# Dealing TensorE's score matmuls out in a fixed order around the gate matmuls

## The chip, the core and the metric

The kernel runs on one core of a Trainium2 chip. The metric is the device time of one execution in microseconds; lower is better. The engines are TensorE (PE in the profile; PEld is its weight load), VectorE (DVE), ScalarE (ACT), GpSimd (POOL), and SyncE (SP), which only issues transfers here. An engine takes its own instructions in the order in which they stand in its queue; what can be reordered is done when the program is built.

## The reference

One decoder layer for 512 tokens of width 1024. The part that matters is the expert mixer at its end (`xb` is the normed input, `T` tokens, 8 heads, 128x128 single-neuron experts, top 16 of them per head):

```python
q = (xb @ w_query).reshape(t, 8, 2, 128)
scores = jnp.einsum("thpc,hpkc->thpk", q, sk)
s1, i1 = lax.top_k(scores[:, :, 0], 16)
s2, i2 = lax.top_k(scores[:, :, 1], 16)
cand = s1[..., :, None] + s2[..., None, :]         # 256 pairs; idx = i1 * 128 + i2
top_s, top_pos = lax.top_k(cand, 16)
gate = jax.nn.softmax(top_s, axis=-1)
act = gelu(einsum("td,thkd->thk", xb, expert_down[idx]))
out = einsum("thk,thkd->td", gate * act, expert_up[idx])
```

## The kernel before

Of the four blocks of 128 tokens, one gathers its experts' rows. The other three (384 tokens, `TD`) are computed densely, and the change touches them alone. For a row `i` of 128 experts the dense way needs three things: the scores `h = gelu(down_i @ xn)` for 128 experts x 384 tokens, the gates `g` (the softmaxed gate of a token where it chose the expert, else zero), and `acc += (h * g).T @ up_i`. There are 128 such rows.

**Score tiles** (`s_tile`, L623). SyncE loads 512 KB of the down table into `w_raw`; ScalarE rounds it to `w_hi` (L615); GpSimd computes the rest `w_lo = w_raw - w_hi` (L616, `load_pair`); TensorE runs 24 matmuls into `s_ps`, eight steps of three (L125 to L127 through `mm3`); ScalarE applies the gelu into `h_act` or `h_far` (L633, L630). `w_raw`, `w_hi`, `w_lo` and `s_ps` have two buffers each. 46 score tiles are made ahead of the accumulation (`make_ahead`, L639): seven between the query heads (L756), nine more after the last head (L757), thirty during the gates (L806). The other 82 are made during the accumulation.

**Selection.** VectorE finds the top 16 of each head (`topk`), then the softmax runs over VectorE and ScalarE (`softmax`, L705: subtract, `Exp` on ScalarE at L708, sum, reciprocal, multiply into `ex`). Nine transposes on TensorE (L763), three each of `i1a`, `i2a` and `ex`, turn the indices and gates so that a token is a column.

**Gates** (L776 to L806). The 384 tokens are taken four at a time, a quad: 96 quads in twelve groups of eight. For a quad, one-hot matrices `oa` and `ob` are built (128x128 per token, four buffers each): on VectorE (L794, L796), or, for two quads of ten, `oa` on ScalarE (L789, L790, an `Abs` and a `Relu` per token) and `ob` on VectorE (L785). TensorE multiplies them into `g_ps` (L800, four fp32 matmuls, which the profile counts as eight passes; six buffers), and ScalarE copies the result into the staging tile `stg` (L801). `stg` has one buffer and holds a group: after its eighth copy GpSimd copies a small part to `gsb0` (L804), SyncE writes the rest to `gmat` in DRAM (L805, 1984 KB), and only then may the next group's first copy write `stg`.

**Accumulation** (L890 on). For each row `i`, VectorE multiplies `h` by the gates into `w` (L902), `w` is split into `whi` and `wlo`, and TensorE runs 18 matmuls into `acc` (L885). The gates of the first four rows come from `gsb0`, later ones are read back from `gmat`.

**What sets the order.** Nothing in this kernel writes out the order between score matmuls and gate matmuls: a scheduler merges the streams engine by engine with estimates of its own, and the pools decide how far it may run ahead. `tc.issue_after(ins)` puts the instructions traced under it behind `ins` in the queue of `ins`'s engine; it is an order in the queue, not a semaphore wait.

Of the kernel before, what the change touches and what calls it, by code (L numbers as in the profile page):

```python
# [12 lines left out]
AF = mybir.ActivationFunctionType  # L13
# [5 lines left out]
P = 128  # L19
T = 512  # L20
D = 1024
DC = D // P
# [9 lines left out]
NG = 1  # L32
NDT = NTB - NG
TD = NDT * P
TG = 32
NTG = TD // TG
# [4 lines left out]
FAR = 20  # L41
S_QUERY = 7
S_WAIT = 9
AHEAD = RUN + FAR
LEAD = 4
FAR_TILES = [RUN + ((2 * k + 1) * (NK - RUN)) // (2 * FAR) for k in range(FAR)]
# [25 lines left out]
def hymba_peer_block(ctx, tc, consts, x, nmix, w_in, w_ba, conv_w, a_log, dt_bias, dn_w, w_pool, pool_scale,  # L72
                     w_out, nffn, w_q, sub_k, downT, down, up, nfin, out):
    nc = tc.nc
# [5 lines left out]
    ident = cst[:, C_ID:C_ID + P]  # L80
# [41 lines left out]
    def mm3(ps, a, b, first, last):  # L122
        ahi, alo = a
        bhi, blo = b
        nc.tensor.matmul(ps, ahi, bhi, start=first, stop=False)  # L125
        nc.tensor.matmul(ps, ahi, blo, start=False, stop=False)  # L126
        nc.tensor.matmul(ps, alo, bhi, start=False, stop=last)  # L127

    def transpose_split(h, tb, hi, lo, psp):
        for q in range(2):  # L130
# [17 lines left out]
    with ExitStack() as fx:  # L148
# [82 lines left out]
        with tc.tile_pool(name="prep", bufs=1) as pr:  # L231
# [58 lines left out]
            for h in range(DNH):  # L290
                for qk, dst in ((0, qT), (1, kT)):
# [84 lines left out]
        with ExitStack() as f2:  # L376
# [110 lines left out]
            for tb in range(NTB):  # L487
# [32 lines left out]
                for h in range(DNH):  # L520
                    nc.tensor.matmul(ops[:, tsl(h)], d["aq"][:, h], vn[:, h], start=(tb == 0 and h == 0),
                                     stop=(h == 3))
# [96 lines left out]
    def h_slot(i):  # L619
        h_tiles[i] = hp[i % (RUN + 1) >= RA].tile([P, TD], F32, name="h_act")  # L620
        return h_tiles[i]

    def s_tile(i, eng):  # L623
        hi, lo = load_pair(downT[i], eng)
        ps = ps_s.tile([P, 512], F32, name="s_ps")[:, :TD]
        for c in range(DC):
            mm3(ps, (hi[:, c, :], lo[:, c, :]), (xn_hi[:, c, NG * P:], xn_lo[:, c, NG * P:]), c == 0, c == DC - 1)
        if i in FAR_TILES:
            ht = hq.tile([P, TD], F32, name="h_far")
            nc.scalar.activation(ht, ps, AF.Gelu)  # L630
            nc.sync.dma_start(out=hfar[FAR_TILES.index(i)], in_=ht)
        else:
            nc.scalar.activation(h_slot(i), ps, AF.Gelu)  # L633


    ahead = list(range(RUN)) + FAR_TILES
# [2 lines left out]
    def make_ahead(goal):  # L639
        while made[0] < min(goal, AHEAD):  # L640
            s_tile(ahead[made[0]], nc.gpsimd)
            made[0] += 1


    def refill(i):
# [56 lines left out]
            nc.vector.tensor_reduce(dst, oh[:, p], axis=AX.X, op=ALU.add)  # L702
        yield

    def softmax(pool, dst, sc):  # L705
        n = sc.shape[1]
        nc.vector.tensor_sub(dst, sc, sc[:, :, 0:1].broadcast_to([P, n, K]))
        nc.scalar.activation(dst, dst, AF.Exp)  # L708
        sm = pool.tile([P, n], F32, name="sm", bufs=1)
        nc.vector.tensor_reduce(sm, dst, axis=AX.X, op=ALU.add)  # L710
        nc.vector.reciprocal(sm, sm)
        nc.vector.tensor_tensor(dst, dst, sm[:, :, None].broadcast_to([P, n, K]), op=ALU.mult)

    with ExitStack() as fy:
        tk = fy.enter_context(tc.tile_pool(name="tk", bufs=2))
        p_pj = fy.enter_context(tc.tile_pool(name="p_pj2", bufs=2, space=PSUM))
        p_sc = fy.enter_context(tc.tile_pool(name="p_sc", bufs=4, space=PSUM))
        skt = tk.tile([P, 16, NK], F32, name="skt", bufs=1)
        nc.scalar.dma_start(out=skt, in_=sub_k)
        SA = [P, NDT, PH, K]  # L720
        i1a = tk.tile(SA, F32, name="i1a", bufs=1)
        i2a = tk.tile(SA, F32, name="i2a", bufs=1)
        tsa = tk.tile(SA, F32, name="tsa", bufs=1)

        def query(h, eng):
            qh = tk.tile([P, 2, T], F32, name="qh")
            w = [load_pair(w_q[2 * h + p], eng) for p in range(2)]
            ps = [p_pj.tile([P, 512], F32, name="q_ps") for p in range(2)]
            parts = [slice(0, T)] if h else [slice(0, T // 2), slice(T // 2, T)]
            for ts in parts:  # L730
                for p in range(2):
                    for c in range(DC):
                        mm3(ps[p][:, ts], (w[p][0][:, c, :], w[p][1][:, c, :]), (xn_hi[:, c, ts], xn_lo[:, c, ts]),
                            c == 0, c == DC - 1)
            for p in range(2):
                cp = nc.scalar.copy(qh[:, p], ps[p])
            behind[:] = [None, cp.ins]
            sc = tk.tile([P, NDT, 2, NK], F32, name="sc")
            ps = [p_sc.tile([P, 512], F32, name="sc_ps") for _ in range(NTB)]
            for p in range(2):  # L740
                for tb in range(NTB):
                    nc.tensor.matmul(ps[tb][:, p * NK:(p + 1) * NK], qh[:, p, tb * P:(tb + 1) * P],
                                     skt[:, 2 * h + p, :], start=(p == 0), stop=(p == 1))
            for tb in range(NTB):
                nc.scalar.copy(sc0[:, tb, h] if tb < NG else sc[:, tb - NG],
                               ps[tb][:, :2 * NK].rearrange("p (a k) -> p a k", a=2))
            return sc

        sc = query(0, nc.vector)
        for h in range(PH):  # L750
            sc_next = query(h + 1, nc.gpsimd) if h + 1 < PH else None
            for _ in topk(tk, sc, NDT, tsa[:, :, h, :], i1a[:, :, h, :], i2a[:, :, h, :]):
                pass
            sc = sc_next
            if sc is not None:
                make_ahead(h + 1)  # L756
        make_ahead(S_QUERY + S_WAIT)  # L757
        ex = tk.tile(SA, F32, name="ex", bufs=1)
        softmax(tk, ex.rearrange("p b h k -> p (b h) k"), tsa.rearrange("p b h k -> p (b h) k"))
        for src, dst in ((i1a, i1t), (i2a, i2t), (ex, gtt)):  # L760
            ps = p_pj.tile([P, 512], F32, name="q_ps")
            for b in range(NDT):
                nc.tensor.transpose(ps[:, b * P:(b + 1) * P], src[:, b].rearrange("p h k -> p (h k)"), ident)  # L763
            nc.vector.tensor_copy(dst, ps[:, :TD])
            if dst is not i2t:
                nc.scalar.activation(n1t if dst is i1t else ngt, ps[:, :TD], AF.Copy, scale=-1.0)
# [3 lines left out]
    with ExitStack() as fy:  # L770
        hq = fy.enter_context(tc.tile_pool(name="hq", bufs=2))
        gs = fy.enter_context(tc.tile_pool(name="gs", bufs=3))
        p_g = fy.enter_context(tc.tile_pool(name="p_g", bufs=6, space=PSUM))
        gsb0 = gp.tile([P, NTG, GN * TG], F32, name="gsb")
        ng = 0
        for tg in range(NTG):  # L776
            stg = gs.tile([P, NK, TG], F32, name="stg", bufs=1)
            for q in range(TG // 4):
                oa = gs.tile([P, 4, P], F32, name="oa", bufs=4)
                ob = gs.tile([P, 4, P], F32, name="ob", bufs=4)  # L780
                ps = p_g.tile([P, 512], F32, name="g_ps")
                t0 = tg * TG + q * 4
                q4 = [P, 4, P]
                if ng % 10 in A_ACT:
                    nc.vector.tensor_tensor(ob, iota[:, None, :].broadcast_to(q4),  # L785
                                            i2t[:, t0:t0 + 4, None].broadcast_to(q4), op=ALU.is_equal)
                    for u in range(4):
                        t = t0 + u
                        nc.scalar.activation(oa[:, u], iota, AF.Abs, bias=n1t[:, t:t + 1])  # L789
                        nc.scalar.activation(oa[:, u], oa[:, u], AF.Relu, scale=ngt[:, t:t + 1], bias=gtt[:, t:t + 1])  # L790
                else:
                    for u in range(4):
                        t = t0 + u
                        nc.vector.tensor_scalar(ob[:, u], iota, i2t[:, t:t + 1], gtt[:, t:t + 1], op0=ALU.is_equal,  # L794
                                                op1=ALU.mult)
                    nc.vector.tensor_tensor(oa, iota[:, None, :].broadcast_to(q4),  # L796
                                            i1t[:, t0:t0 + 4, None].broadcast_to(q4), op=ALU.is_equal)
                ng += 1
                for u in range(4):
                    nc.tensor.matmul(ps[:, u * P:(u + 1) * P], ob[:, u], oa[:, u], start=(u == 0), stop=(u == 3))  # L800
                nc.scalar.copy(stg[:, :, q * 4:q * 4 + 4].rearrange("p i t -> p t i"),  # L801
                               ps.rearrange("p (t i) -> p t i", i=NK))
            sv = stg.rearrange("p i t -> p (i t)")
            nc.gpsimd.tensor_copy(gsb0[:, tg, :], sv[:, :GN * TG])  # L804
            nc.sync.dma_start(out=gmat[tg, :, GN * TG:], in_=sv[:, GN * TG:])  # L805
            make_ahead(S_QUERY + S_WAIT + (tg + 1) * (AHEAD - S_QUERY - S_WAIT) // NTG)  # L806

    with ExitStack() as fz:
        fin = fz.enter_context(tc.tile_pool(name="fin", bufs=1))
# [182 lines left out]
```

## Time and profile before

| | us |
|---|---|
| median of three runs | 1635.62 (1633.59 to 1635.65) |
| the profiled execution | 1633.33, of which the span of the trace is 1631.6 |
| TensorE busy | 1550.3 (95%) |
| VectorE, ScalarE, GpSimd busy | 1258.6, 706.1, 573.1 |
| from the last query to the first `acc` matmul | about 431.5 to 746.5 on the span |

The span starts with the first instruction of the trace; all times in the text are counted from there. "Busy" adds up instruction times, so an engine can be busy and slow (TensorE at a lower clock), or idle for a short stretch that a share of the whole span hides. For that the profile is read by stage: how long TensorE stood in a stretch, and which engine's event ended the wait.

### The profile page before, as it was taken

How to read it: one execution, taken by the hardware profiler on the slowest of the kernel's cores; microseconds unless marked ns; L12 is line 12 of the kernel's file. 1: busy time of each engine (PE TensorE's matmuls, PEld its weight loads, DVE VectorE, ACT ScalarE, POOL GpSimd, SP SyncE). 2: the span in 40 equal slices, each digit the busy share in tenths (PEclk: the TensorE clock that was granted, in tenths of full speed). 3: DMA queues.
4: the chain of work that ended last, by engine and by line, in shares of the span. 5: the costliest groups of instructions: out<-in, count | busy, mean ns of one | idle time of the engine just before them, and what ended most of it. 6: DMA issues, size and time to landing. Idle time of an engine off the chain costs nothing.

```text
span 1631.6 us, 23412 instructions
## 1 busy us (share of the span) xinstructions
PE 1550.3 (95%) x8417; PEld 1393.4 (85%) x8417; DVE 1258.6 (77%) x2666; ACT 706.1 (43%) x1097; POOL 573.1 (35%) x389
## 2 busy tenths in 40 slices
PE   6999999999949899999999999999999999999996
PEld 5888898888948888889888898888888888888885
DVE  5576646799967666668989888788888888888985
ACT  5545344333326877773333333333333333333333
POOL 2003230144433333330045444455444444444431
PEclk9999999999979999999999999999999999999998
DMA  6221221423313445557589989999999999999982
GB/s 205 78 65 54 66 79 40 161 90 98 92 52 128 165 174 189 189 189 240 171 309 344 388 309 344 349 333 328 336 344 340 323 338 333 337 322 347 335 274 88
DMA packets 140661, 364.97 MB, mean 224 GB/s; under 512 B 11040, under 2 KB 63792, under 8 KB 138880
## 3 DMA queue, kind: packets, MB, share of 16 engines
q1 hardware_dynamic: 102544, 224.98, 39.8%
q0 software_dynamic: 37856, 137.44, 23.2%
q8 instruction: 66, 1.08, 0.3%
q10 hardware_dynamic: 144, 1.05, 0.2%
q14 instruction: 51, 0.42, 0.1%
HBM read 330.40 MB, written 33.03 MB: 223 GB/s over the span
## 4 chain that ended last, share of the span: by engine, by line
PE 84%; DVE 6%; issue 4%; DMA 3%; ACT 2%; POOL 1%; SPq 0%; ACTq 0%; DVEq 0%; POOLq 0%
PE acc L885 30%; PE s_ps L127 10%; PE s_ps L125 10%; PE s_ps L126 10%; PE pj L125 3%; PE pj L126 3%; PE pj L127 3%; PE g_ps L800 2%; PE q_ps L126 2%; PE q_ps L127 2%; PE q_ps L125 2%; DVE ob L794 1%; ACT stg L801 1%; PE ups L435 1%; PE p L444 1%
## 5 line engine op out<-in xcount | busy, mean ns | idle before, releaser
L125 PE MATMUL s_ps<-xn_hi,w_hi 128*128 128x384 f32 x1024 | 351.7, 343 | 20.4 <-ACT h_act L633 20.1
L127 PE MATMUL s_ps<-xn_hi,w_lo 128*128 128x384 f32 x1024 | 348.1, 340 | 2.9 <-POOL w_lo L616 2.9
L126 PE MATMUL s_ps<-xn_lo,w_hi 128*128 128x384 f32 x1024 | 347.9, 340 | 0.0
L615 ACT ACTIVATE w_hi<-w_raw 128x1024 fp32r<-128x1024 f32 x144 | 152.6, 1060 | 322.4 <-PE s_ps L126 234.6
L860 POOL DMA_INDIRECT row<-in_down_dram,eidx x128 | 180.8, 1413 | 263.3 <-DVE row L862 160.2
L869 POOL DMA_INDIRECT row<-in_up_dram,eidx x128 | 177.1, 1383 | 211.6 <-DVE xr L871 183.9
L885 PE MATMUL acc<-u_lo,whi 128*128 128x512 f32 x768 | 237.7, 389 | 2.1 <-DVE u_lo L120 2.1
L885 PE MATMUL acc<-u_hi,whi 128*128 128x512 f32 x768 | 238.4, 391 | 0.0
L885 PE MATMUL acc<-u_hi,wlo 128*128 128x512 f32 x768 | 237.4, 389 | 0.0
L616 POOL TENSOR_TENSOR w_lo<-w_raw,w_hi 128x1024 fp32r<-128x1024 f32 x60 | 149.1, 2486 | 244.2 <-ACT w_hi L615 216.8
L125 PEld LDWEIGHTS s_ps<-xn_hi,w_hi 128*128 128x128 f32 x1024 | 193.7, 189 | 24.3 <-ACT h_act L633 20.4
L127 PEld LDWEIGHTS s_ps<-xn_hi,w_lo 128*128 128x128 f32 x1024 | 193.7, 189 | 3.8 <-POOL w_lo L616 3.8
L119 ACT ACTIVATE whi<-w 128x384 fp32r<-128x384 f32 x128 | 67.1, 525 | 298.5 <-issue 250.3
L126 PEld LDWEIGHTS s_ps<-xn_lo,w_hi 128*128 128x128 f32 x1024 | 193.6, 189 | 3.2
L862 DVE SCALAR_TENSOR_TENSOR row<-row,xg 128x1024 f32<-128x1024 f32 x128 | 153.2, 1221 | 26.8 <-DMA row<-in_down_dram,eidx 26.5
L885 PEld LDWEIGHTS acc<-u_lo,whi 128*128 128x128 f32 x768 | 144.1, 188 | 34.1 <-DVE u_lo L120 3.2
L871 DVE SCALAR_TENSOR_TENSOR xr<-row,dots,xr 128x1024 f32<-128x1024 f32 x128 | 164.3, 1283 | 10.0 <-DMA row<-in_up_dram,eidx 8.2
L885 PEld LDWEIGHTS acc<-u_hi,wlo 128*128 128x128 f32 x768 | 144.1, 188 | 30.0
L120 DVE TENSOR_TENSOR u_lo<-u_raw,u_hi 128x1024 fp32r<-128x1024 f32 x128 | 156.3, 1221 | 10.1 <-ACT u_hi L119 10.1
L885 PEld LDWEIGHTS acc<-u_hi,whi 128*128 128x128 f32 x768 | 143.0, 188 | 23.7 <-ACT u_hi L119 0.2
L794 DVE TENSOR_SCALAR ob<-cst,i2t,gtt 128x128 f32<-128x128 f32 x308 | 109.6, 416 | 56.2 <-PE g_ps L800 56.2
L119 ACT ACTIVATE u_hi<-u_raw 128x1024 fp32r<-128x1024 f32 x128 | 134.6, 1051 | 38.0 <-DMA u_raw<-in_up_dram 34.8
(300 smaller groups left out, 2421.0 us busy)
## 6 DMA issues: line engine op xcount, KB each, us to landing
u_raw<-in_up_dram SPq DMA_DIRECT2D x128, 512.0 KB, 5.9
w_raw<-in_downT_dram SPq DMA_DIRECT2D x128, 512.0 KB, 5.4
gmat<-stg SPq DMA_DIRECT2D x12, 1984.0 KB, 7.0
gsb<-gmat SPq DMA_DIRECT2D x31, 768.0 KB, 8.2
w_raw<-in_w_in_dram SPq DMA_DIRECT2D x20, 512.0 KB, 3.6
w_raw<-in_w_q_dram SPq DMA_DIRECT2D x16, 512.0 KB, 3.6
w_raw<-in_w_out_dram SPq DMA_DIRECT2D x8, 512.0 KB, 3.6
hfar<-h_far SPq DMA_DIRECT2D x20, 192.0 KB, 3.7
```

Of the source, the lines that this page charges most:

```text
L119: nc.scalar.activation(hi, src, AF.Copy)
L120: nc.vector.tensor_sub(lo, src, hi.bitcast(F32))
L125: nc.tensor.matmul(ps, ahi, bhi, start=first, stop=False)
L126: nc.tensor.matmul(ps, ahi, blo, start=False, stop=False)
L127: nc.tensor.matmul(ps, alo, bhi, start=False, stop=last)
L615: nc.scalar.activation(hi, raw, AF.Copy)
L616: eng.tensor_sub(lo, raw, hi.bitcast(F32))
L860: nc.gpsimd.indirect_dma_start(out=r, out_offset=None, in_=down, in_offset=bass.IndirectOffsetOnAxis(ap=eidx[b][:, s:s + 1], axis=0))
L862: nc.vector.scalar_tensor_tensor(r, r, 1.0, xg, op0=ALU.mult, op1=ALU.mult, accum_out=dots[:, s:s + 1])
L869: nc.gpsimd.indirect_dma_start(out=r, out_offset=None, in_=up, in_offset=bass.IndirectOffsetOnAxis(ap=eidx[b][:, s:s + 1], axis=0))
L871: nc.vector.scalar_tensor_tensor(xr[b], r, dots[:, s:s + 1], xr[b], op0=ALU.mult, op1=ALU.add)
L885: nc.tensor.matmul(acc[b][n], l[:, bs], r[:, n * 512:(n + 1) * 512], start=(i == 0 and l is whi and r is uhi), stop=(i == NK - 1 and l is ...
```

## The change

Three things are done. First, the softmax's `Exp` is queued on ScalarE behind the gelu of the last of the nine score tiles, and the transposes on TensorE behind that tile's last matmul. Second, the thirty score tiles of the gate stage become a stream of steps (one step is three matmuls, eight are a tile); `take` hands out the next steps, and every step and every quad's matmuls is put behind the TensorE instruction before it, so that TensorE's order is fixed: 16 steps first (`S_FIRST`), then after each quad two or three steps until the 240 are used up. Third, the load and split of the next score tile are traced when the first step of the current one is taken.

```diff
+S_FIRST = 16
...
-    def s_tile(i, eng):
-        hi, lo = load_pair(downT[i], eng)
+    def s_steps(i, pair):
+        hi, lo = pair
         ps = ps_s.tile([P, 512], F32, name="s_ps")[:, :TD]
         for c in range(DC):
-            mm3(ps, (hi[:, c, :], lo[:, c, :]), (xn_hi[:, c, NG * P:], xn_lo[:, c, NG * P:]), c == 0, c == DC - 1)
+            s_last[0] = mm3(ps, (hi[:, c, :], lo[:, c, :]), (xn_hi[:, c, NG * P:], xn_lo[:, c, NG * P:]), c == 0,
+                            c == DC - 1)
+            if c < DC - 1:
+                yield
...
+    def ahead_steps():
+        pair = load_pair(downT[ahead[made[0]]], nc.gpsimd)
+        while made[0] < AHEAD:
+            i, now = ahead[made[0]], pair
+            made[0] += 1
+            for k, _ in enumerate(s_steps(i, now)):
+                if not k and made[0] < AHEAD:
+                    pair = load_pair(downT[ahead[made[0]]], nc.gpsimd)
+                yield
...
-        nc.scalar.activation(dst, dst, AF.Exp)
+        with tc.issue_after(behind.ins) if behind is not None else ExitStack():
+            nc.scalar.activation(dst, dst, AF.Exp)
...
-        softmax(tk, ex.rearrange("p b h k -> p (b h) k"), tsa.rearrange("p b h k -> p (b h) k"))
+        softmax(tk, ex.rearrange("p b h k -> p (b h) k"), tsa.rearrange("p b h k -> p (b h) k"), s_act[0])
...
+            with tc.issue_after(s_last[0].ins):
+                for b in range(NDT):
+                    pe_last = nc.tensor.transpose(ps[:, b * P:(b + 1) * P], src[:, b].rearrange("p h k -> p (h k)"),
+                                                  ident)
...
+        def take(goal):
+            nonlocal taken, pe_last
+            while taken < goal:
+                with tc.issue_after(pe_last.ins):
+                    next(steps, None)
+                pe_last = s_last[0]
+                taken += 1
+
+        n_steps = (AHEAD - S_QUERY - S_WAIT) * DC
+        take(S_FIRST)
...
+                with tc.issue_after(pe_last.ins):
+                    for u in range(4):
+                        pe_last = nc.tensor.matmul(ps[:, u * P:(u + 1) * P], ob[:, u], oa[:, u], start=(u == 0),
+                                                   stop=(u == 3))
+                take(S_FIRST + ng * (n_steps - S_FIRST) // (TD // 4))
...
-            make_ahead(S_QUERY + S_WAIT + (tg + 1) * (AHEAD - S_QUERY - S_WAIT) // NTG)
```

**ScalarE around the `Exp`.** These are its rows before, after the last query head; `w_hi` and `h_act` belong to score tiles.

```order
L615 ACTIVATE w_hi<-w_raw 128x1024
L633 ACTIVATE h_act<-s_ps 128x384
L615 ACTIVATE w_hi<-w_raw 128x1024
L633 ACTIVATE h_act<-s_ps 128x384
L708 ACT_TABLE_LOAD
L708 ACTIVATE ex<-ex 128x384
L615 ACTIVATE w_hi<-w_raw 128x1024
L633 ACT_TABLE_LOAD
L633 ACTIVATE h_act<-s_ps 128x384
```

And these are the rows of the change at the end of the tenth score tile behind the last query.

```order
L616 ACTIVATE w_hi<-w_raw 128x1024
L638 ACTIVATE h_act<-s_ps 128x384
L616 ACTIVATE w_hi<-w_raw 128x1024
L638 ACTIVATE h_act<-s_ps 128x384
L732 ACT_TABLE_LOAD
L732 ACTIVATE ex<-ex 128x384
L792 ACTIVATE n1t<-q_ps 128x384
L792 ACTIVATE ngt<-q_ps 128x384
```

The `Exp` and its table load moved to the end of this stage's score tiles: eight gelus that stood behind it now stand ahead of it.

**TensorE around the transposes.** Before, with 240 score matmuls (ten tiles) ahead of the first row shown here:

```order
L763 MATMUL q_ps<-cst,i1a 128x128 x3
L763 MATMUL q_ps<-cst,i2a 128x128 x3
L125 MATMUL s_ps<-xn_hi,w_hi 128x384
L126 MATMUL s_ps<-xn_lo,w_hi 128x384
L127 MATMUL s_ps<-xn_hi,w_lo 128x384
L125 MATMUL s_ps<-xn_hi,w_hi 128x384
L126 MATMUL s_ps<-xn_lo,w_hi 128x384
L127 MATMUL s_ps<-xn_hi,w_lo 128x384
L763 MATMUL q_ps<-cst,ex 128x128 x3
```

Of the change, with the same 240 ahead:

```order
L788 MATMUL q_ps<-cst,i1a 128x128 x3
L788 MATMUL q_ps<-cst,i2a 128x128 x3
L788 MATMUL q_ps<-cst,ex 128x128 x3
L126 MATMUL s_ps<-xn_hi,w_hi 128x384
L127 MATMUL s_ps<-xn_lo,w_hi 128x384
L128 MATMUL s_ps<-xn_hi,w_lo 128x384
```

The transposes of `ex` lost the six score matmuls in front of them. From there to the first gate matmul 48 score matmuls stand now, where 10 stood.

**TensorE inside the gates.** Before, at the end of the stage, the last three pieces of gate work:

```order
L800 MATMUL g_ps<-oa,ob 128x128 x22
L125 MATMUL s_ps<-xn_hi,w_hi 128x384
L126 MATMUL s_ps<-xn_lo,w_hi 128x384
L800 MATMUL g_ps<-oa,ob 128x128 x6
L127 MATMUL s_ps<-xn_hi,w_lo 128x384
L800 MATMUL g_ps<-oa,ob 128x128 x4
```

Of the change, at the start of the stage:

```order
L841 MATMUL g_ps<-oa,ob 128x128 x4
L126 MATMUL s_ps<-xn_hi,w_hi 128x384
L127 MATMUL s_ps<-xn_lo,w_hi 128x384
L128 MATMUL s_ps<-xn_hi,w_lo 128x384
L126 MATMUL s_ps<-xn_hi,w_hi 128x384
L127 MATMUL s_ps<-xn_lo,w_hi 128x384
L128 MATMUL s_ps<-xn_hi,w_lo 128x384
L841 MATMUL g_ps<-oa,ob 128x128 x4
```

This pattern, with six or nine score matmuls between two quads, runs through all 96 quads. Between the last gate matmul and the first `acc` matmul stand 12 score matmuls now; before, 69.

**ScalarE between two groups.** Of the change, from a late copy of the fourth group to the first copies of the fifth (L829 and L830 build `oa`):

```order
L844 COPY stg<-g_ps 128x4x128
L616 ACTIVATE w_hi<-w_raw 128x1024
L635 ACTIVATE h_far<-s_ps 128x384
L844 COPY stg<-g_ps 128x4x128
L829 ACTIVATE oa<-cst,n1t 128x128 x2
L830 ACTIVATE oa<-oa,gtt,ngt 128x128 x2
L829 ACTIVATE oa<-cst,n1t 128x128 x2
L830 ACTIVATE oa<-oa,gtt,ngt 128x128
L616 ACTIVATE w_hi<-w_raw 128x1024
L635 ACTIVATE h_far<-s_ps 128x384
L830 ACTIVATE oa<-oa,gtt,ngt 128x128
L844 COPY stg<-g_ps 128x4x128 x6
```

ScalarE's own order also moved, since the scheduler places its work around TensorE's new one: splits and gelus stand singly between the copies, where before they came in runs.

## Rows read from the trace of the kernel before

**Rows 1.** The page: its first line, and one transfer with its us to landing.

```profile
span 1631.6 us, 23412 instructions
...
u_raw<-in_up_dram SPq DMA_DIRECT2D x128, 512.0 KB, 5.9
```

**Rows 2.** A window of the accumulation: busy us (instructions) per engine, clock, DMA.

```profile
860.00:960.00 100.00, 100.00 (x492) 89.35 (x491) 86.12 (x128) 36.59 (x50) 50.11 (x36) 1.00 0.97 356
```

**Rows 3.** Waits from 425 to 505: engine, line, releaser, total, times, longest.

```profile
DVE i1t L764 <- PE q_ps L763: 24.1, 1, 24.1
...
PE s_ps L125 <- ACT h_act L633: 20.1, 1, 20.1
```

**Rows 4.** Timeline of ScalarE, 436 to 504: start, us, instruction, idle time before it.

```profile
441.62 1.28 ACT L708 ACT_TABLE_LOAD   x1
465.45 0.52 ACT L708 ACTIVATE ex<-ex 128x384 f32<-128x384 f32 x1 [22.55 <-DVE ex L707]
...
489.49 1.06 ACT L615 ACTIVATE w_hi<-w_raw 128x1024 fp32r<-128x1024 f32 x1 [2.79 <-PE s_ps L126]
490.45 0.47 ACT L633 ACTIVATE h_act<-s_ps 128x384 f32<-128x384 f32 x1
493.71 1.06 ACT L615 ACTIVATE w_hi<-w_raw 128x1024 fp32r<-128x1024 f32 x1 [2.78 <-PE s_ps L126]
```

**Rows 5.** Timeline of TensorE: the first score matmul behind the last query.

```profile
431.56 0.42 PE L125 MATMUL s_ps<-xn_hi,w_hi 128*128 128x384 f32 x1
```

**Rows 6.** The tile `q_ps`: durations ns min/median/max, first and last start.

```profile
L763 PE MATMUL q_ps<-cst,i1a x3: 271/272/273, 497.9 to 498.1; 128*128 128x128 f32 x3
...
L763 PE MATMUL q_ps<-cst,ex x3: 270/271/272, 499.6 to 499.8; 128*128 128x128 f32 x3
```

**Rows 7.** Timeline of VectorE: the rest of the softmax.

```profile
468.50 0.55 DVE L710 TENSOR_REDUCE sm<-ex 128x24 f32<-128x384 f32 x1
...
471.54 0.29 DVE L711 RECIPROCAL sm<-sm 128x24 f32<-128x24 f32 x1
...
472.56 0.93 DVE L702 TENSOR_REDUCE i2a<-oh 128x48 f32<-128x768 bf16 x1
473.42 0.84 DVE L712 TENSOR_TENSOR ex<-ex,sm 128x384 f32<-128x384 f32 x1
```

**Rows 8.** Windows around two pauses of TensorE; the clock is third from the end.

```profile
472.00:475.00 3.00, 3.00 (x11) 3.00 (x10) 2.26 (x3) 0.00 (x0) 1.85 (x1) 0.50 0.59 165
475.00:478.00 3.00, 3.00 (x19) 3.00 (x18) 0.00 (x0) 1.19 (x2) 0.05 (x1) 0.98 0.42 164
536.00:538.00 2.00, 0.59 (x2) 0.26 (x2) 0.00 (x0) 2.00 (x7) 1.95 (x1) 1.00 1.16 492
540.00:542.00 2.00, 2.00 (x8) 2.00 (x7) 0.00 (x0) 0.00 (x0) 1.94 (x1) 0.50 0.75 248
```

**Rows 9.** The tile `g_ps`: its copies, durations ns, first and last start.

```profile
L801 ACT COPY stg<-g_ps x96: 1036/1094/1227, 503.7 to 734.7; 128x512 f32<-128x512 f32 x96
```

**Rows 10.** The chain that ended last: start, us, what.

```profile
519.77 7.06 DMA gmat<-stg
...
526.91 7.74 ACT stg L801 x8
...
561.76 0.91 PE g_ps L800 x8
...
746.47 4.11 PE acc L885 x18
```

**Rows 11.** Timeline of ScalarE: half of a quad's `oa`.

```profile
519.94 0.70 ACT L789 ACTIVATE oa<-cst,n1t 128x128 f32<-128x128 f32 x2
520.52 0.89 ACT L790 ACTIVATE oa<-oa,gtt,ngt 128x128 f32<-128x128 f32 x2
```

**Rows 12.** The transfers of L805: from issue to landing.

```profile
DMA to landing us min/median/max: 6.0/7.0/8.4
```

**Rows 13.** Timeline of all engines behind the last group's last copy.

```profile
734.73 1.16 ACT L801 COPY stg<-g_ps 128x512 f32<-128x512 f32 x1
...
735.95 0.29 POOL L804 COPY gsb<-stg 128x128 f32<-128x128 f32 x1 [7.61 <-ACT stg L801]
...
736.87 0.52 ACT L119 ACTIVATE whi<-w 128x384 fp32r<-128x384 f32 x1 [0.98 <-DVE w L902]
```

More of the change, by code (lines that the diff above doesn't have):

```diff
@@ L126, in mm3 @@
         nc.tensor.matmul(ps, ahi, blo, start=False, stop=False)
-        nc.tensor.matmul(ps, alo, bhi, start=False, stop=last)
+        return nc.tensor.matmul(ps, alo, bhi, start=False, stop=last)
     def transpose_split(h, tb, hi, lo, psp):
@@ L621, in h_slot, with s_tile @@
         return h_tiles[i]
-    def s_tile(i, eng):
-        hi, lo = load_pair(downT[i], eng)
+    def s_steps(i, pair):
+        hi, lo = pair
         ps = ps_s.tile([P, 512], F32, name="s_ps")[:, :TD]
         for c in range(DC):
-            mm3(ps, (hi[:, c, :], lo[:, c, :]), (xn_hi[:, c, NG * P:], xn_lo[:, c, NG * P:]), c == 0, c == DC - 1)
+            s_last[0] = mm3(ps, (hi[:, c, :], lo[:, c, :]), (xn_hi[:, c, NG * P:], xn_lo[:, c, NG * P:]), c == 0,
+                            c == DC - 1)
+            if c < DC - 1:
+                yield
         if i in FAR_TILES:
             ht = hq.tile([P, TD], F32, name="h_far")
-            nc.scalar.activation(ht, ps, AF.Gelu)
+            s_act[0] = nc.scalar.activation(ht, ps, AF.Gelu)
             nc.sync.dma_start(out=hfar[FAR_TILES.index(i)], in_=ht)
         else:
-            nc.scalar.activation(h_slot(i), ps, AF.Gelu)
+            s_act[0] = nc.scalar.activation(h_slot(i), ps, AF.Gelu)
+        yield
+    s_last, s_act = [None], [None]
+    def s_tile(i, eng):
+        for _ in s_steps(i, load_pair(downT[i], eng)):
+            pass
     ahead = list(range(RUN)) + FAR_TILES
@@ L642, in make_ahead @@
             made[0] += 1
+    def ahead_steps():
[6 more added lines that the diff above has]
+                    pair = load_pair(downT[ahead[made[0]]], nc.gpsimd)
+                yield
     def refill(i):
@@ L703, in topk, with softmax @@
         yield
-    def softmax(pool, dst, sc):
+    def softmax(pool, dst, sc, behind=None):
         n = sc.shape[1]
         nc.vector.tensor_sub(dst, sc, sc[:, :, 0:1].broadcast_to([P, n, K]))
-        nc.scalar.activation(dst, dst, AF.Exp)
+        with tc.issue_after(behind.ins) if behind is not None else ExitStack():
+            nc.scalar.activation(dst, dst, AF.Exp)
         sm = pool.tile([P, n], F32, name="sm", bufs=1)
@@ L758, in hymba_peer_block @@
         ex = tk.tile(SA, F32, name="ex", bufs=1)
-        softmax(tk, ex.rearrange("p b h k -> p (b h) k"), tsa.rearrange("p b h k -> p (b h) k"))
+        softmax(tk, ex.rearrange("p b h k -> p (b h) k"), tsa.rearrange("p b h k -> p (b h) k"), s_act[0])
         for src, dst in ((i1a, i1t), (i2a, i2t), (ex, gtt)):
             ps = p_pj.tile([P, 512], F32, name="q_ps")
-            for b in range(NDT):
-                nc.tensor.transpose(ps[:, b * P:(b + 1) * P], src[:, b].rearrange("p h k -> p (h k)"), ident)
+            with tc.issue_after(s_last[0].ins):
+                for b in range(NDT):
+                    pe_last = nc.tensor.transpose(ps[:, b * P:(b + 1) * P], src[:, b].rearrange("p h k -> p (h k)"),
+                                                  ident)
             nc.vector.tensor_copy(dst, ps[:, :TD])
@@ L774, in hymba_peer_block @@
         gsb0 = gp.tile([P, NTG, GN * TG], F32, name="gsb")
+        steps = ahead_steps()
+        taken = 0
+        def take(goal):
[7 more added lines that the diff above has]
+        take(S_FIRST)
         ng = 0
@@ L798, in hymba_peer_block @@
                 ng += 1
-                for u in range(4):
-                    nc.tensor.matmul(ps[:, u * P:(u + 1) * P], ob[:, u], oa[:, u], start=(u == 0), stop=(u == 3))
+                with tc.issue_after(pe_last.ins):
[3 more added lines that the diff above has]
+                take(S_FIRST + ng * (n_steps - S_FIRST) // (TD // 4))
                 nc.scalar.copy(stg[:, :, q * 4:q * 4 + 4].rearrange("p i t -> p t i"),
```

## The prediction

> **What bounds the kernel now.** The windows come first, because the share of busy time over the whole span hides the stages. In the accumulation TensorE is busy in every microsecond at full clock [rows 2], so whatever brings the first `acc` matmul forward, which starts at 746.5 [rows 10], should come off the end one for one. The stage ahead of it is where TensorE stands. The list of waits there has two entries that are one story: a score matmul waited 20.1 for a gelu, and VectorE's copy of the transposed indices 24.1 for TensorE's transposes [rows 3]. ScalarE's timeline names the cause: its `Exp` stood at the head of the queue for 22.55 until VectorE had selected the last head's experts, and the gelus behind it could not free `s_ps` [rows 4]. In the gates nothing stands out in this way; there the question is which engine sets the period of a group of eight quads. From the first copy to `stg` (503.7) to the last one's start (734.7) [rows 9] and end (735.9 [rows 13]) the stage takes 232.2, or 19.3 a group.
>
> **Step 1, the ten score tiles and the `Exp`.** The first score matmul behind the last query runs at 431.6 [rows 5]. A tile's period is 493.71 - 489.49 = 4.22 where nothing is in its way [rows 4], which is 0.176 a matmul. With the `Exp` behind them ten tiles end at 431.6 + 42.2 = 473.8, and the transposes of `i1a` and `i2a` follow, where they now start at 497.9 [rows 6]: 24.1 earlier. VectorE is just in time: in this trace the last index was reduced from 472.56 to 473.5 [rows 7]. GpSimd's six further splits now run beside the selection; I leave that at nothing, since a microsecond or two of delay there only goes into the next wait.
>
> **Step 2, the wait that comes in.** The transposes of `ex` now stand directly behind, with no score matmul between, and their softmax can only start when the tenth gelu has run. Taken in a row: about 0.2 until the last matmul is out, gelu 0.47, table load 1.28, `Exp` 0.52 [rows 4], sum 0.55, reciprocal 0.29, product 0.84 [rows 7], and some 0.1 for each of five handovers: 4.6 from 473.8, so 478.4. TensorE has six transposes for 0.7 of it and then stands 3.9; before, it had score matmuls there, so it stood for none of this. Queued behind the waiting transposes are all score steps and with them the gates.
>
> The clock has a price here as well. After the long pause it was 0.50 until about 475 and 0.98 behind [rows 8]: some 6 us of work at half speed, 3 lost. A short pause did it too: between 536 and 538 TensorE was busy for only 0.59, and at 540 to 542 it ran at 0.50 [rows 8]. I take 3 for the new pause; the ends are nothing and 3.1. The Trainium skill, "TensorE: Matmul & The Clock Gate", "HAM oscillation — how this bites in real kernels", warns that a loop which lets TensorE pause again and again has part of its matmuls at half clock. By that rule the change would pay for the new pause, and for any that the fixed order adds among the quads; the trace agrees as far as the 0.50 above goes. Without any loss of clock the sum below would be 4 better.
>
> **Step 3, the start of the gates.** After the transposes (0.3) come 48 score matmuls, 8.4, plus the 3: the first quad starts at 490.1. Its eight passes take 0.91 [rows 10], and its copy starts some 0.4 later, at 491.4 instead of 503.7. The 16 steps are no loss, as they are taken out of the later work; VectorE has them as cover to build the first quads.
>
> **Step 4, the period of a group.** Three candidates. *TensorE*: 64 passes at 0.114 [rows 10] are 7.3, 56 score matmuls at 0.176 are 9.9, together 17.2. *ScalarE*: eight copies 7.74 [rows 10]; two and a half tiles at 1.43 (split and gelu, 489.49 to 490.92 [rows 4]) 3.6; 1.6 quads whose `oa` it builds, at twice 1.35 to 1.45 [rows 11], 4.4: together 15.7. *The staging tile*: after the eighth copy `stg` is free again only when the write to `gmat` has landed, 7.06 and some handover, 7.2 from the copy's end to the next copy [rows 10]. ScalarE's other 8.0 costs nothing where it stands in that wait, and lengthens the group where it stands between the copies. The rows of the change show a group's end with a split, a gelu and a whole `oa` in the wait; counted over the ten middle groups the order has about 4.0 in the wait and 3.7 between the copies. So ScalarE's round is 7.2 + 7.7 + 3.7 = 18.6, longer than TensorE's 17.2, and I take it. The bounds are 17.2 and the present 19.3. Twelve rounds without the last wait are 12 x 18.6 - 7.2 = 216, so the last copy ends at 707.4 instead of 735.9.
>
> **Step 5, the way into the accumulation.** From the last copy's end, through GpSimd's copy, the product and the split, to `whi` is 735.9 to 737.4, 1.5 [rows 13]. Before, 69 score matmuls hid it (TensorE only turned to `acc` at 746.5); now 12 are left, so it lies open: first `acc` at 708.9, with 1 lost to another dip of the clock, 709.9 in effect. That is 36.6 before 746.5. SyncE's queue has the third and fourth rows' `u_raw` behind the first read-back of `gmat`, which waits for the last write: landed at 714.7, then 5.9 for `u_raw` [rows 1], 721, and two splits of about 1.1 each, 723. The third row is due at 709 + 2 x 4.1 + 45 x 0.176 = 725. It holds with 2 to spare; I take off 0.6 for what may be lost there.
>
> **The sum.** The first copy comes 12.3 earlier (24.1, less 3.9 standing, 3 of clock and 38 more score matmuls ahead of the gates, 6.7; the rest is that the present order also waits there a little). The groups give 232.2 - 216 = 16.2, the end 10.6 - 1.5 - 1 = 8.1: 36.6, less 0.6 is 36. From the profiled execution, 1633.3 (span 1631.6 [rows 1] and 1.7 around it), that leaves 1597. The three runs have a median 2.3 above the profiled one; I give 1599 for the median of the changed kernel.
>
> **Rivals.**
> *A: ScalarE keeps up, TensorE bounds the gates at 17.2.* Last quad done at 490.1 + 206, copy and chain 2.9: first `acc` at 699, 47 earlier, 1587. For it: ScalarE's work alone is 15.7. Against it: the 7.2 comes round in every group, and only six `g_ps` buffers (13 us of TensorE's work) bridge it.
> *B: the round stays at 19.3.* Then 491.4 + 232.2 + 1.5 = 725: 21 earlier, 1613. For it: a fixed order cannot turn to score matmuls when an `oa` of ScalarE's is late, and each pause may cost clock. The slowest write, 8.4 [rows 12], would by itself put 1.3 on a group.
> *C: slower.* ScalarE finds all its other work between the copies: 7.2 + 15.7 = 22.9 a group, 12 x 22.9 - 7.2 = 268, first `acc` at 760, 14 later, 1649. It decides from a round of 21.7, where the gates take back all that was gained ahead. Against it stand the rows of the change, in which about half of that work lies in the wait.
> *D: nothing gained.* The topk, slowed by GpSimd's splits, holds the transposes, or the accumulation's start stalls on its loads, until the 36 are used up; no row has a stall of that size.
>
> **How the numbers follow.** Chances: the forecast, 1592 to 1606, 0.60; A 0.14; B 0.17; C 0.05; D 0.04. The 8-in-10 range reaches to A's and B's centres: 1587 to 1613. 0.2% (3.3 us) is about what a measurement of this kernel can tell from no change. Faster by more than that: 0.92; within: 0.03; slower: 0.05.
>
> **What would show it.** Right: no wait of the score matmuls between 440 and 474, the `Exp` with no long idle time before it, one pause of about 4 ahead of the `ex` transposes with clock 0.50 behind; copies of `stg` with a group period near 18.6 and "gmat" as the releaser of each group's first copy; first `acc` near 710, and TensorE full from there. Wrong: a period of 17.2 with no wait for `gmat` (A), waits of `g_ps` for ScalarE's `oa` in many groups (B, C), or pauses of `acc` for `u_raw` in the first rows.

## The result and the profile after

The changed kernel takes 1615.79 us (median of four runs, 1614.37 to 1618.58) against 1634.61 beside it (1633.23 to 1635.65): ratio 0.9887, interval 0.9869 to 0.9906, 18.8 us faster. The forecast was 1599, with 1587 to 1613 as its range: about half of the forecast gain came. The profiled execution was the slowest of the four, 1618.58, with a span 14.8 shorter than before's [rows 1].

The chain of waits can be walked stage by stage. Ahead of the gates, the waits of TensorE from 425 to 505 and the tile `q_ps` (durations ns min/median/max, first and last start), changed kernel:

```profile
PE q_ps L788 <- DVE i1a L725: 2.9, 1, 2.9
PE q_ps L788 <- DVE ex L736: 2.1, 1, 2.1
```

```profile
L788 PE MATMUL q_ps<-cst,i1a x3: 273/273/329, 477.1 to 477.4; 128*128 128x128 f32 x3
L788 PE MATMUL q_ps<-cst,i2a x3: 272/272/329, 478.0 to 478.3; 128*128 128x128 f32 x3
L788 PE MATMUL q_ps<-cst,ex x3: 421/422/446, 480.7 to 481.1; 128*128 128x128 f32 x3
```

The 20.1 and the 24.1 of [rows 3] are gone and the transposes come 20.8 earlier than in [rows 6], but TensorE stands twice: for the indices, which were taken to be ready, and for `ex`. The transposes of `ex` run at half clock (421 ns against 272; the granted clock was 0.50 from 480 to 486). Next, the copies to `stg` with what ScalarE waited for ahead of them, and first, last and three other issues of the write to `gmat`, from SyncE's timeline; the third view is ScalarE's timeline where the next group's first copy waited for such a write:

```profile
L844 ACT COPY stg<-g_ps x96: 997/1109/1192, 493.3 to 718.6; 128x512 f32<-128x512 f32 x96
its engine sat idle before it (us, times) until:
  DMA gmat<-stg: 29.2, 9
```

```profile
509.40 0.33 SPq L848 DMA_DIRECT2D gmat<-stg  x1
...
545.47 0.42 SPq L848 DMA_DIRECT2D gmat<-stg  x1
567.39 0.33 SPq L848 DMA_DIRECT2D gmat<-stg  x1
585.43 0.32 SPq L848 DMA_DIRECT2D gmat<-stg  x1
...
719.68 0.32 SPq L848 DMA_DIRECT2D gmat<-stg  x1
```

```profile
554.73 2.97 ACT L844 COPY stg<-g_ps 128x512 f32<-128x512 f32 x3 [6.12 <-DMA gmat<-stg]
574.60 5.77 ACT L844 COPY stg<-g_ps 128x512 f32<-128x512 f32 x6 [3.19 <-DMA gmat<-stg]
594.10 4.64 ACT L844 COPY stg<-g_ps 128x512 f32<-128x512 f32 x5 [4.82 <-DMA gmat<-stg]
```

The first group runs from 493.3 to 509.4, 16.1; the other eleven take (719.68 - 509.40) / 11 = 19.1 each. From issue to the copy behind it the write takes 7.2 (567.39 to 574.60), but also 9.3 (545.47 to 554.73) and 8.7 (585.43 to 594.10); over the nine that ScalarE waited for, the mean is 7.9. In the same places TensorE stands for an `oa` of ScalarE's that is queued behind the waiting copy; of TensorE's waits from 485 to 722 this is the largest:

```profile
PE g_ps L841 <- ACT oa L830: 9.2, 10, 3.0
```

One of these waits on its timeline, and windows around it (granted clock third from the end):

```profile
600.43 0.49 PE L841 MATMUL g_ps<-oa,ob 128*128 128x128 f32 x2 [3.03 <-ACT oa L830]
```

```profile
604.00:607.40 3.40, 3.40 (x12) 3.40 (x13) 1.72 (x5) 1.26 (x2) 0.72 (x1) 0.50 0.66 276
607.40:612.00 4.60, 4.60 (x30) 4.60 (x29) 2.87 (x5) 4.13 (x11) 2.38 (x1) 0.84 0.92 376
```

Last, the accumulation. The chain that ended last has the first `acc` at 721.21, and the waits of TensorE from 715 on show what came in:

```profile
721.21 5.95 PE acc L927 x18
```

```profile
PE acc L927 <- DVE u_lo L121: 7.3, 3, 3.0
PE acc L927 <- ACT whi L120: 2.8, 1, 2.8
```

The first `acc` is 25.3 earlier than in [rows 10], but the span is only 14.8 shorter. Where the other 10 went is in VectorE's and TensorE's timelines around 810, and in windows there:

```profile
804.22 0.29 DVE L897 SCALAR_TENSOR_TENSOR eidx<-i,i 128x128 int32<-128x128 f32 x1
...
813.01 1.23 DVE L904 SCALAR_TENSOR_TENSOR row<-row,xg 128x1024 f32<-128x1024 f32 x1 [6.89 <-DMA row<-in_down_dram,eidx]
...
815.79 1.22 DVE L121 TENSOR_TENSOR u_lo<-u_raw,u_hi 128x1024 fp32r<-128x1024 f32 x1
```

```profile
817.06 1.22 PE L927 MATMUL acc<-u_lo,whi 128*128 128x512 f32 x2 [2.98 <-DVE u_lo L121]
832.72 0.74 PE L927 MATMUL acc<-u_lo,whi 128*128 128x512 f32 x2 [1.37 <-DVE u_lo L121]
844.36 1.21 PE L927 MATMUL acc<-u_lo,whi 128*128 128x512 f32 x2 [3.00 <-DVE u_lo L121]
```

```profile
800.00:820.00 20.00, 17.02 (x77) 14.59 (x76) 13.11 (x23) 6.98 (x10) 9.02 (x7) 0.93 0.70 228
...
840.00:860.00 20.00, 17.00 (x75) 14.48 (x74) 17.03 (x27) 7.00 (x9) 10.97 (x9) 0.91 0.93 333
```

```profile
817.00:820.00 3.00, 2.94 (x7) 2.36 (x8) 3.00 (x7) 0.00 (x0) 2.40 (x2) 0.52 0.92 285
...
834.00:836.00 2.00, 2.00 (x10) 1.66 (x9) 1.09 (x3) 0.00 (x0) 1.02 (x1) 1.00 1.03 416
...
844.00:847.00 3.00, 2.64 (x6) 2.15 (x7) 3.00 (x6) 0.00 (x0) 0.81 (x1) 0.57 0.92 320
```

From the first `w` (720.04) VectorE selects experts for the other token block and writes `eidx` at 804.22. Only then can rows be gathered; VectorE stands 6.89 for the first, with the split of `u` that TensorE needs queued behind it. TensorE then waits three times. Behind the two waits of about 3 the granted clock was 0.52 and 0.57; behind the one of 1.37 it stayed at 1.00. The kernel before has the same knot: its row product waits 4.89 ahead of 828.01, and TensorE's two waits for `u_lo`, which end at 830.90 and 840.40, were in the trace all along, just ahead of the window of [rows 2]. VectorE's timeline, and TensorE's waits from 715 to 900:

```profile
828.01 1.22 DVE L862 SCALAR_TENSOR_TENSOR row<-row,xg 128x1024 f32<-128x1024 f32 x1 [4.89 <-DMA row<-in_down_dram,eidx]
```

```profile
PE acc L885 <- DVE u_lo L120: 2.1, 2, 1.2
```

There VectorE's first `w` (736.3) came 10 ahead of the first `acc` (746.3), because the 69 score matmuls stood between; that lead was the cover, as the experiments bear out. Now it is 1.2. VectorE's first `w`, before and then in the changed kernel:

```profile
736.28 1.03 DVE L902 TENSOR_TENSOR w<-h_act,gsb 128x384 f32<-128x384 f32 x2 [3.23 <-POOL gsb L804]
```

```profile
720.04 1.03 DVE L944 TENSOR_TENSOR w<-h_act,gsb 128x384 f32<-128x384 f32 x2 [2.15 <-POOL gsb L847]
```

### The profile page after: what moved, and what is told of

It is laid out like the page before. It is cut to its first block, busy times and chain, and to the rows that moved or that the text cites. A ratio compares the mean times of both kernels' runs of the same rounds, so it can differ in the third digit from the quotient of the medians.

```text
span 1616.8 us, 23439 instructions
## 1 busy us (share of the span) xinstructions
PE 1553.2 (96%) x8417; PEld 1399.9 (87%) x8417; DVE 1285.1 (79%) x2666; ACT 705.3 (44%) x1097; POOL 577.7 (36%) x389
## 4 chain that ended last, share of the span: by engine, by line
PE 74%; DVE 13%; ACT 5%; DMA 4%; issue 3%; POOL 1%; SPq 0%; ACTq 0%; DVEq 0%; POOLq 0%
PE acc L927 31%; PE s_ps L126 8%; PE s_ps L127 8%; PE s_ps L128 8%; PE pj L127 3%; PE pj L126 3%; ACT stg L844 3%; PE g_ps L841 3%; PE pj L128 3%; DMA gmat<-stg 2%; PE ups L436 1%; DVE rep L678 1%; PE p L445 1%; DMA row<-in_down_dram,eidx 1%; DVE oh L718 1%
## 5 line engine op out<-in xcount | busy, mean ns | idle before, releaser
L126 PE MATMUL s_ps<-xn_hi,w_hi 128*128 128x384 f32 x1024 | 358.3, 350 | 0.2 <-ACT h_far L635 0.2
L617 POOL TENSOR_TENSOR w_lo<-w_raw,w_hi 128x1024 fp32r<-128x1024 f32 x60 | 154.5, 2576 | 293.1 <-ACT w_hi L616 257.1
L834 DVE TENSOR_SCALAR ob<-cst,i2t,gtt 128x128 f32<-128x128 f32 x308 | 121.9, 457 | 34.6 <-PE g_ps L841 34.3
```

What stands on the lines that cost most here:

```text
L617: eng.tensor_sub(lo, raw, hi.bitcast(F32))
```

## The experiments

The first theory was this: the gates end 12 later than forecast, the staging tile being slower than priced, and 10 more are given back behind the first `acc` because VectorE has lost its lead. Rivals: the gates are held by TensorE; the loss at the end is general overload or chance.

**The changed kernel again.** No edit.

> The changed kernel once more, as the mark for the runs beside it: 1614 to 1618. Theory: a gates stage whose group period is near 19 and whose first group takes 16, and some 10 us given back behind the first acc, as in its first trace; if the 10 us are an accident of that one execution, this trace has no wait of acc for u_lo above 2 in total and a span some 5 shorter.

1615.07; ratio 0.9882 (0.9866 to 0.9897). First group 16.1, the others 19.0, waits for `u_lo` 6.5 in all. Not an accident.

**The softmax and transposes alone.** The new gates loop taken back:

```
...
-                with tc.issue_after(pe_last.ins):
-                    for u in range(4): pe_last = nc.tensor.matmul(...)
-                take(S_FIRST + ng * (n_steps - S_FIRST) // (TD // 4))
+                for u in range(4): nc.tensor.matmul(...)
...
+            make_ahead(S_QUERY + S_WAIT + (tg + 1) * (AHEAD - S_QUERY - S_WAIT) // NTG)
```

> Only the Exp behind nine tiles and the three transposes behind the tenth; the gates as the scheduler places them. Theory (the two parts add up, and what the scheduler's gates hide at the end stays hidden): the first copy to stg some 10 to 12 earlier than in the kernel before, group period still near 19.5, first acc 10 to 12 earlier, nearly all of it kept behind it: 1622 to 1626. Rival (the whole gain is the fixed order's): 1632 to 1635. Rival (the scheduler lets the score tiles take what was won): 1630 or more, first copy earlier but first acc within 4 of before.

1618.12; ratio 0.9892 (0.9877 to 0.9907). More than expected: the first copy comes at 489.4, 14 earlier, the last `gmat` issue at 720.4, and the first `acc` at 730.8, 10 behind it as before. Neither the theory's 1622 to 1626 nor a rival's range came: nearly the whole gain of the change, 17.0 of 20.0, is this part's. What the changed kernel has in addition, a first `acc` 9.6 earlier, is worth 2 to 3 at the end. From here on the theory was that the end hangs on VectorE's work, which starts with the last copy.

**The fixed order in the gates alone.** `Exp` without its `behind`, the transposes without their `issue_after`.

> Only the fixed order in the gates; Exp and transposes where the scheduler puts them. Theory: first copy near 504 as before, first group 16, the others near 19.1, first acc about 15 earlier than 746.5, and about 10 of that given back in waits of acc for u_lo with half clock behind them: 1627 to 1632. Rival (nothing is given back behind the first acc when the stage ahead is as before): 1618 to 1621.

1632.59; ratio 0.9984 (0.9974 to 0.9994). First copy at 510.4, not near 504 (the 16 first steps stand ahead of it), first group 16.1, the others 19.1, last issue at 736.8: the fixed order does not bring the last copy forward at all. Its shorter rounds only pay for the later start. It does bring the first `acc` to 738.4, 8 earlier where 15 was expected; the waits for `u_lo` are 6.2, and 2.5 remain. With the 17.0 of the other part that is 19.5 of the 20.0 that both give together. The time lies just above the theory's 1627 to 1632; the rival of 1618 to 1621 is out.

**The transposes behind one more tile.**

```
+        make_ahead(S_QUERY + S_WAIT + 1)
         for src, dst in ((i1a, i1t), (i2a, i2t), (ex, gtt)):
-S_FIRST = 16
+S_FIRST = 8
```

> Exp still behind nine tiles, but all three groups of transposes behind the eleventh, and 8 first steps where there were 16: the same score matmuls ahead of the first quad. Theory: the waits for i1a (2.9) and ex (2.1) and the half clock (2.5) ahead of the first quad go, which starts 6 to 8 earlier, near 485, and everything behind moves with it: 1607 to 1611. Rival (VectorE sets the start of the quads, since it finished the indices late and has less time for the first oa and ob): a wait of g_ps for DVE takes their place, 1614 to 1617.

1610.66; ratio 0.9846 (0.9832 to 0.9859), 4.4 below the changed kernel beside it. The waits for `i1a` and `ex` are gone, and the granted clock was 1.00 from 470 to 492. The first quad starts at 486.3, against 490.8 and 491.9 in the two traces of the changed kernel, a little less than the 6 to 8 expected; the first copy is at 487.7, the last issue at 714.5. No wait for VectorE's one-hot matrices took the place of those that went: the start of the quads is TensorE's.

**The row products later, in the changed kernel and in the one before.** In `gathers`, three gathers go out ahead of the first product, then six empty steps (two and a half rows of the accumulation):

```
+                late = []
...
+                    late.append((r, s))
+                    if s == 2:
+                        for _ in range(6): yield
+                    while late and (len(late) > 3 or s == NSLOT - 1):
+                        r, k = late.pop(0)
...
-                    nc.vector.scalar_tensor_tensor(r, r, 1.0, xg, ..., accum_out=dots[:, s:s + 1])
+                        nc.vector.scalar_tensor_tensor(r, r, 1.0, xg, ..., accum_out=dots[:, k:k + 1])
...
-        n_g = NG * (2 * NSLOT + PH // 2 * 7)
+        n_g = NG * (2 * NSLOT + PH // 2 * 7 + 6)
```

> The changed kernel with VectorE's first product on a gathered row put two and a half rows of the accumulation later, behind the splits of u that follow (three gathers are issued first, then six empty steps). Theory (the end hangs on VectorE: the time from the last copy to the end is 895 to 898 in all six traces so far, because the first gathered row, due when the selection is done, holds VectorE with the splits of u behind it): the wait of acc for u_lo falls from 7 to under 2, its half clock goes with it, from the last copy to the end some 887 to 890, 1606 to 1609. Rival (VectorE simply has too much to do in these 130 us): the waits for u_lo only come at other rows, 1614 to 1617.

> The same edit in the kernel before, where TensorE comes to acc 10 behind the last copy and stands for u_lo 2.1 in all. Theory: only these 2 to 3 can be won, 1631 to 1633. Rival (the edit is worth the same anywhere): 8 less than before, 1626 to 1628.

Changed kernel: 1604.77; ratio 0.9815 (0.9801 to 0.9829), 10.3 below the changed kernel without the edit, a little less than the 1606 to 1609 expected. No `acc` waits for `u_lo`; from 800 to 860 TensorE is busy throughout, at full clock:

```profile
800.00:860.00 60.00, 60.00 (x299) 53.96 (x298) 47.35 (x70) 20.78 (x29) 29.91 (x20) 1.00 0.93 327
```

Kernel before: 1631.69; ratio 0.9979 (0.997 to 0.9988), 3.4 below the kernel before and within the 1631 to 1633 expected. VectorE is busy for as long as without the edit (1287.1 against 1285.1 in the changed kernel, 1259.2 against 1258.6 in the one before), so it did not have too much to do; the place of the row products in its queue was the cost.

**Two staging tiles, and the kernel to compare them with (the mark).** To make room, `RUN = 19` and `FAR = 27` (26 and 20 before) in both; one of them also has

```
-            stg = gs.tile([P, NK, TG], F32, name="stg", bufs=1)
+            stg = gs.tile([P, NK, TG], F32, name="stg", bufs=2)
```

> The changed kernel with two staging tiles; to make room, seven more score tiles go through DRAM (19 instead of 26 stay in the SBUF). Theory (the group's round is landing 7.9, copies 7.7 and 3.5 between them, 19.1): no copy waits for the write any more, the period falls to TensorE's own, 17.2 to 17.7, the last copy comes 15 to 20 earlier than beside it with one staging tile, and the end 12 to 18: 1597 to 1604. Rival (TensorE sets the period, by waits for ScalarE's oa and half clock that stay): period 18.5 or more, 1609 to 1616.

> The mark for the two staging tiles: one tile, and 19 score tiles in the SBUF as there. If the seven further round trips cost nothing: 1613 to 1618, period near 19.1. If they load SyncE's queue and the DMA engines so that the writes land later: period up to 20, 1622.

Two tiles: 1590.87; ratio 0.9729 (0.9715 to 0.9742). One: 1617.46; ratio 0.9887 (0.9871 to 0.9902). The second is within the 1613 to 1618 that was expected if the further round trips cost nothing. Between them lie 26.6, more than the 12 to 18 expected: TensorE's own pace turned out faster than the 17.2 to 17.7 taken for it, and nothing of the earlier start was given back (from the first `acc` to the end 893.3 with two tiles, 895.5 with one). First and last issue of the write with two tiles, and the longest of ScalarE's waits from 490 to 700:

```profile
510.51 0.33 SPq L848 DMA_DIRECT2D gmat<-stg  x1
...
696.23 0.32 SPq L848 DMA_DIRECT2D gmat<-stg  x1
```

```profile
ACT stg L844 <- PE g_ps L841: 23.3, 32, 1.4
```

No copy waits for the write; the copies now wait for TensorE. The period is (696.23 - 510.51) / 11 = 16.9, against 19.2 with one tile, and the last issue is 24.8 earlier than there (721.02). The rival, that TensorE holds the period by waits and half clock of its own, is out: TensorE's waits for `oa`, 9.6 with one tile here, are gone too, so they came from the staging tile.

**No splits on GpSimd beside the selection.**

```
+            s_tile(ahead[made[0]], None if made[0] >= S_QUERY else nc.gpsimd)
...
+        if eng is None: return hi, hi
```

> The changed kernel without GpSimd's splits for the nine tiles behind the last queries' (that subtraction is left out, the high part is multiplied in place of the low one, so the scores of nine tiles are less exact). Theory (the selection on VectorE is slowed where its long instructions run beside a split): the transposes of i1a start 2.5 to 3.5 earlier, at 473.5 to 474.5, with no wait for DVE i1a above 0.5, the second instruction of the one-hot stays near 1.76 and 1.81, and the end follows: 1611 to 1613.5. Rival (the selection itself is late, or waits for its scores): i1a as before at 476.5 to 477, 1614 to 1617.

1612.24; ratio 0.986 (0.9845 to 0.9875). The tile `q_ps`, and VectorE's two instructions of the one-hot over 436 to 478 (x count, busy, mean ns), without the splits and then in the changed kernel:

```profile
L790 PE MATMUL q_ps<-cst,i1a x3: 271/272/272, 473.3 to 473.5; 128*128 128x128 f32 x3
```

```profile
L720 DVE TENSOR_TENSOR oh<-fij,cst 128x1536 bf16<-128x1536 f32 x2 | 3.5, 1758 | 0.1
...
L723 DVE TENSOR_TENSOR oh<-oh,idf 128x1536 bf16<-128x1536 bf16 x2 | 1.9, 959 | 0.1
```

```profile
L718 DVE TENSOR_TENSOR oh<-fij,cst 128x1536 bf16<-128x1536 f32 x2 | 5.8, 2883 | 0.1
...
L721 DVE TENSOR_TENSOR oh<-oh,idf 128x1536 bf16<-128x1536 bf16 x2 | 4.0, 2000 | 0.1
```

The indices are ready 3.8 earlier and the wait for `i1a` is gone. Only the wait for `ex` stays, now 3.4. The price of the splits, which the forecast set to nothing, is about 3 at the end (2.8 by the medians, 3.6 by the ratios to the kernel before); the intervals of the two ratios overlap, so this size is less sure than the 3.8.

**Each part alone, with the row products later.**

> The softmax part alone, with VectorE's row products two and a half rows later. Theory (behind the first acc all kernels need 884, and what is lost beyond that grows as the lead of VectorE over TensorE shrinks; here it has 10): first acc near 731, 1613 to 1616. Rival (the edit wins 10 wherever the gates start earlier): 1607 to 1609.

> The fixed order in the gates alone, with the row products two and a half rows later. Theory: the fixed order won some 8 to 9 at the first acc (738.4 against 746.5), which the wait for the first gathered row hid; now it shows: 1621 to 1625. Rival (the fixed order wins nothing, however the row products stand): 1630 to 1633.

Softmax part: 1615.83; ratio 0.9883 (0.9868 to 0.9898). Gates part: 1621.57; ratio 0.9919 (0.9905 to 0.9932). Both fall into the theory's bounds. So the medians of the kernels with one part, both, or none are (the kernel before, run beside them, was between 1634.0 and 1635.1 throughout)

| | neither | softmax | gates | both |
|---|---|---|---|---|
| row products as they were | 1635.1 | 1618.1 | 1632.6 | 1615.1 |
| row products later | 1631.7 | 1615.8 | 1621.6 | 1604.8 |

The gates part is worth 2.5 to 3.0 in the first line and 10.1 to 11.0 in the second.

**Two staging tiles, later transposes, later row products.**

> The changed kernel with two staging tiles, the transposes behind the eleventh tile, and the row products later. Theory (the three lie behind one another on the path): first acc near 693, 884 behind it, 1577 to 1581. Rival (with the quads at TensorE's pace VectorE or ScalarE becomes late for them when they start earlier): 1582 to 1590.

1574.29; ratio 0.9628 (0.9615 to 0.9641), 60 below the kernel before and nearly 3 below the 1577 to 1581 expected; the first `acc` is at 690.9. All that TensorE waits for from 470 to 900:

```profile
PE q_ps L789 <- DVE i2t L791: 0.8, 1, 0.8
PE acc L935 <- ACT whi L120: 0.6, 1, 0.6
PE s_ps L128 <- POOL w_lo L617: 0.5, 1, 0.5
PE g_ps L842 <- ACT oa L831: 0.3, 1, 0.3
```

The profiles of all these runs agree on one number, the time from the first `acc` to the end of the span. It is 885 to 888 where VectorE's lead is 10 (before, softmax alone), 893 to 896 where it is 1.2 (the changed kernel, gates alone, later transposes, one or two staging tiles, no splits), and 882 to 884 with the row products later, whatever the lead. Counted from the issue of the last write, where VectorE's work of this stage begins, the nine traces without the later row products all need 895 to 898: in them the end follows the last copy, and bringing `acc` closer behind it is worth 2 to 3 at most.

## Why the prediction was wrong

**The first paragraph, "one for one".** This is the step whose mechanism failed. That TensorE is full from 860 to 960 [rows 2] says nothing of 800 to 860, where the kernel before stood 2.1 for `u_lo`: it had no slack there, so an earlier start without an earlier VectorE could only lengthen that wait. In the profiled execution 9.2 of the miss lie behind the first `acc`. From there to the end it took 895.6, the kernel before 885: 5.2 of the difference is longer standing for `u_lo` (7.3 against 2.1), 1.8 is in the first 18 `acc` matmuls (5.95 against 4.11 [rows 10], with a granted clock of 0.50 from 722 to 724), and the rest, some 3, is the lower clock behind the two waits of about 3. Step 5 looked for a loss in the loads of `u_raw` and took off 0.6, and rival D named the place ("the accumulation's start stalls on its loads") but dismissed it because "no row has a stall of that size". The row to look for was a small stall with a covered cause. The last write is issued 16.2 earlier (719.68 against 735.91), and the span is 14.8 shorter: the gain followed the last copy, not the first `acc`.

**Step 4, the period.** The mechanism holds: nine of eleven groups begin with a wait for the write, and with a second tile those waits are gone. The sign that rivals B and C named, waits of `g_ps` for ScalarE's `oa`, came as well, but as a consequence of the waiting copy. Two sizes were off. The write with its handover took 7.9 in the mean where 7.2 was put in, the rest between the copies 3.5 where it was 3.7, so the round is 19.1, not 18.6: 5.7 over eleven groups. And the first group waits for no write. It ran at TensorE's pace, 16.1 from its first copy to its last, where "twelve rounds without the last wait" gave it 11.4: 4.7 more. Before the change it took the same, from 503.7 [rows 9] to 519.77 [rows 10], so the rows had this number. TensorE's own pace is 16.9 a group (17.2 forecast). What held the groups before was something else: only one copy waited for the write there, for 4.1, and TensorE waited for VectorE's `oa` instead (its waits from 503 to 750):

```profile
PE g_ps L800 <- DVE oa L796: 18.3, 19, 1.7
```

The fixed order did away with these waits and came up against the staging tile, and so the period, from issue to issue of the write, only went from 19.6 to 19.1.

**Steps 1 to 3.** The ten tiles ran without a wait, as forecast, and this part brought most of the gain. "I leave that at nothing" for the splits was wrong: the transposes of `i1a` came 3.3 after the forecast 473.8. The wait for `ex` and the half clock came as described, but as the indices were late, less of the wait was left (2.1, not 3.9). In all TensorE stood 5.3 there in three pieces where 3.9 was put in, and this is most of the 1.9 by which the first copy was late: the one error hid part of the other. The Trainium skill, "SBUF — State Buffer", "Who interferes with whom", says that a VectorE instruction with two inputs in the SBUF and a GpSimd instruction that reads the SBUF exclude each other, one standing until the other has run. The trace agrees: without the splits the first instruction of the one-hot takes 1758 ns each time, in the changed kernel 1.76 and 4.01, and the one of 4.01 started at 471.10 together with a split of 2.40, as the timelines of VectorE and GpSimd show:

```profile
471.10 4.01 DVE L718 TENSOR_TENSOR oh<-fij,cst 128x1536 bf16<-128x1536 f32 x1
```

```profile
471.10 2.40 POOL L617 TENSOR_TENSOR w_lo<-w_raw,w_hi 128x1024 fp32r<-128x1024 f32 x1 [1.81 <-ACT w_hi L616]
```

**Step 5.** From the last copy's end to the first `acc` the path took the 1.5 forecast (719.7 to 721.2). The 1 for a dip of the clock was 1.8. What the path uncovered was not only itself, but the loss of VectorE's lead.

**The sum.** 1.9 at the start, 4.7 and 5.7 in the groups, 9.2 behind the first `acc`: 21.5 of the 21.6 by which the profiled execution, 1618.6, missed its 1597. By parts, the forecast gave 16.2 to shorter groups and 8.1 to the end. In fact the fixed order moved the last copy by less than 1 (720.4 with the softmax part alone, 719.7 with both), and the 10 that it won at the first `acc` were given back but for 2 to 3.

## What to carry to other kernels

A stage in which the bound engine is full says only that it is full there. Before an earlier start is counted one for one, look for the first wait behind it, however small, and ask what lead the feeding engine has and whether the change takes it. When work that covers a wait is moved forward, follow each engine that used the time, not only the one that did the covered work. A count of rounds needs its first round priced by itself, since what the rounds wait for is not there yet.

## What the runs showed of the hardware

TensorE stood 7.3 in three pieces of 1.4 to 3.0 behind the first gathered rows, and this cost about 10 (10.3 by the medians with and without the later row products). The rest is reduced clock, 0.93 and 0.91 in windows of 20, and it followed the two pauses of 2.98 and 3.00 (granted clock 0.52 and 0.57), while behind the one of 1.37 it stayed at 1.00. In the gates it was 0.50 from 604.0 to 607.4, behind a pause of 3.03 and three short ones. The Trainium skill, "TensorE: Matmul & The Clock Gate", "HAM oscillation — how this bites in real kernels", says that matmuls which come in bursts with pauses between them run in part at half clock, again behind each pause; the trace agrees for the pauses of about 3, and the kernel without them (two staging tiles, later transposes, later row products) has a mean granted clock of 0.996 against 0.987.
